# A feed-forward in two passes, its first product by seven block products, its middle layer in memory

## The chip, the cores and the metric

The kernel runs on one core of a Trainium2 chip. The metric is the device time of one execution in microseconds. The kernel before took 4279.12 us, the median of three runs (4273.91 to 4280.19).

## The reference, cut to what matters

The reference is a stack of two blocks of the first kind (layers 0 and 1) and one of a second kind with experts. 1024 tokens of width 1024 pass through all of them; 256 context tokens pass through layer 0. Everything is float32. A block of the first kind mixes the tokens (windowed attention, a gating unit, a Fourier mix, then the product with `w_out`), and ends in a feed-forward of width 4096. The scale, shift and gate vectors of each block come from a product of a condition vector with `w_ada`.

```
def squared_relu_mlp(h, w1, w2):
    return jnp.square(jax.nn.relu(h @ w1)) @ w2

for l in range(DEPTH):                      # DEPTH = 2
    mod_x = (silu(c) @ w_ada[l] + b_ada[l])
    sh1, sc1, g1, sh2, sc2, g2 = jnp.split(mod_x, 6, axis=-1)
    ...
    x = x + g1 * rmsnorm(y, g_post_mix[l])  # y: mixers, then @ w_out
    hx2 = rmsnorm(x, g_pre_ff[l]) * (1.0 + sc2) + sh2
    x = x + g2 * rmsnorm(squared_relu_mlp(hx2, w_ff1[l], w_ff2[l]), g_post_ff[l])
    # the same for the context h_ctx, in layer 0 alone
```

## The kernel before, in words

Every float32 matrix is split into a high part (`hi`, rounded to fp32r) and the rest (`lo`). A product is three matmuls: high by high, high by low, low by high (`mm3`). A split is a copy for `hi` (`copy` picks ScalarE or VectorE, `split` takes ScalarE) and a subtraction for `lo` (VectorE in `lo`; `lo_any` may pick GpSimd).

The order of all instructions on all engines is fixed at build time by a planner. Pieces of work are Python generators (`Sched.spawn`, with a priority; a lower number goes first); a `yield` of a condition holds a piece back until the planner's `Model` says that operands, buffers and banks are there. `Model` gives each instruction a time by a formula in `Engine.cost` (on VectorE 0.07 us and 0.00104 us per column, a DMA its bytes at 359 GB/s and 2 us). On the chip each engine then works through its list in that order and waits for semaphores; SP issues nearly all DMAs, also in order.

On-chip buffers: 46 blocks of 128x1024 float32 (`blk`), 7 half blocks (`hb`), 8 PSUM banks of 128x512. `room(n)`, `roomh(n)` and `banks(n)` ask whether n are free. `Weights` streams a list of weight tiles: load a block by SP, split it into two blocks, free the first.

`out_proj` multiplies each tile of 128 tokens by `w_out`, adds the residual, normalizes, transposes the result and stores the split transpose in `ffx`, the operand of the feed-forward: 4 row groups x 2 token halves x (hi, lo) = 16 blocks for the 1024 tokens, 4 for the context. When it is done, `ff` begins.

`ff` goes over groups of 128-column chunks of the middle layer (32 chunks; in layer 0 groups of two and a last one of four, in layer 1 groups of four). For each chunk and token half (512 tokens) it does 8 row blocks x 3 matmuls of 512 columns into one bank, and for the context 24 of 256 columns; `relu2` applies relu and square on ScalarE and splits the result into a block on the chip. Then, per token tile and 512 output columns, the group's chunks are multiplied by `w_ff2` into a bank, and VectorE adds the bank to an accumulator block. In the last group each finished tile goes to `finisher`: norm, residual, the next block's norm, transposes, split. The next block's input products follow at once.

`mod_dve` makes the modulation vectors that are needed later: a half of 512 columns is eight multiply-adds on VectorE for each of one or two vectors, with weights that SP loads into half blocks. It starts when layer 0's `out_proj` is over and runs beside the feed-forward.

Of the kernel before, what the change touches and what calls it, by code (L numbers as in the profile page):

```python
# [19 lines left out]
P = 128  # L20
# [12 lines left out]
FRES = 16  # L33
QLIM = 9
FLIM = 6
DEPTH = 3
# [10 lines left out]
GROUPS = [cuts(*[2]*14+[4]), cuts(*[4]*8)]  # L47
# [30 lines left out]
MG = 1  # L78
# [20 lines left out]
LB = 0.5  # L99
TP = 1  # L100
# [260 lines left out]
class Base:  # L361
    def __init__(self, ctx, tc, a):
        self.ctx, self.tc, self.a = ctx, tc, a
        self.m = Model()
        self.nc = NC(tc.nc, self.m)
        self.s = Sched(self.m)
        tp = lambda **k: ctx.enter_context(tc.tile_pool(**k))
        self.heap = tp(name="heap", bufs=1)
        self.small = tp(name="small", bufs=1)
        self.psum = tp(name="psum", bufs=NBANK, space=bass.MemoryType.PSUM)  # L370
        self.dram = tp(name="dram", bufs=1, space=bass.MemoryType.DRAM)
        self.rsv = 0
        self.bias = BIAS
        self.lbias = LB
        self.fstage = self.routing = 0
        self.slots = dict(blk=[0.0] * NBLK, hb=[0.0] * NHB, ps=[0.0] * NBANK)
# [226 lines left out]

class Seq:
# [11 lines left out]
class Block1(Base):  # L616
# [827 lines left out]
    def ff_dst(self, S, t):  # L1444
        X = S.ffx
        def dst(half):
            if S.ctx:
                return [(slice(0, 512), X[half][0][:, :, t * P:(t + 1) * P], X[half][1][:, :, t * P:(t + 1) * P])]
            out = []
            for i in range(2):  # L1450
                hi, lo = X[2 * half + i][t // 4]
                c = (t % 4) * P
                out.append((slice(i * 256, (i + 1) * 256), hi[:, :, c:c + P], lo[:, :, c:c + P]))
            return out
        return dst

    def out_proj(self, seqs, W, l, src, dst):
# [34 lines left out]
        def back(i, x, ys):  # L1492
            S, t = tiles[i]
            yield lambda: S.ctx in par
            G, A, B = par[S.ctx]
            yield from self.post(x, ys, G)
            self.unbank(*ys)
            nc.sync.dma_start(dst[S.ctx][t * P:(t + 1) * P, :], x)
            yield lambda: self.room(1)
            z = yield from self.prenorm(x, A, B)  # L1500
            self.free(x)
            S.odone += 1
            if S.odone == S.n:
                self.free(G, A, B)
            yield lambda: S.ctx or S.ffx[0][t // 4] is not None
            yield from self.transpose_split(z, self.ff_dst(S, t))
            self.free(z)
            S.ffdone.add(t)

        def halves():  # L1510
            for i in range(2):
                yield lambda: self.room(8 if dropped else 15) and (dropped if i else X.fourd)
                for kp in X.ffx:
                    kp[i] = tuple(self.blk((P, 2, 512), F32R) for _ in range(2))
# [4 lines left out]
        for i, (S, t) in enumerate(tiles):  # L1519
            if t == 0:  # L1520
# [3 lines left out]
                else:  # L1524
                    if len(seqs) == 2:
                        self.s.spawn(params(S), 1, "params")
                    S.ffx = [[None, None] for _ in range(4)]
# [16 lines left out]
        yield lambda: X.ffx[0][1] is not None  # L1544
# [3 lines left out]
    def ff_items(self, l, groups):  # L1548
        w1, w2 = self.a["w_ff1"][l], self.a["w_ff2"][l]
        it = []  # L1550
        for r in groups:
            it += [(("1", c), w1[:, c * P:(c + 1) * P].rearrange("(k p) f -> p k f", p=P), (P, KC, P)) for c in r]
            it += [(("2", c), w2[c * P:(c + 1) * P, :], (P, 1024)) for c in r]
        return it

    def relu2(self, ps, n, out, done, key):
        nc = self.nc
        yield lambda: self.roomh(1)
        r = self.hb()
        nc.scalar.activation(r[:, :n], ps[:, :n], AF.Relu)  # L1560
        self.unbank(ps)
        nc.scalar.activation(r[:, :n], r[:, :n], AF.Square)
        yield
        self.copy(out[:, 0, :n], r[:, :n])
        yield
        self.lo(out[:, 1, :n], r[:, :n], out[:, 0, :n])
        self.freeh(r)
        done.add(key)

    def ff(self, seqs, W, groups, fin, last_group):  # L1570
# [4 lines left out]
        need = lambda r: 2 * len(r) + (len(r) // 2 if C else 0)  # L1575
        yield lambda: self.room(10 if C else 8)
        acc = {(S.ctx, t): self.blk() for S in seqs for t in range(S.n)}
        done = set()
        self.ff_acc = 0
        hs = self.ff_h  # L1580
        for g, cs in enumerate(groups):
            last = g == len(groups) - 1
            parts = [(0, 0), (0, 1)] + ([(1, 0)] if C else [])
            order = [(c, p) for c in cs for p in parts] if g else [(c, p) for p in parts for c in cs]
            uses = {c: 0 for c in cs}
            for c, p in order:
                S, hb = seqs[0] if p[0] else X, p[1]
                nt = range(4 * hb, 4 * hb + 4) if not S.ctx else range(2)
                hk = (c - c % 2, "c") if S.ctx else (c, hb)
                yield lambda: W.has(("1", c)) and self.banks(2) and (hk in hs or self.room(1)) and all(t in S.ffdone for t in nt)  # L1590
                w1 = W.ready["1", c]
                ps = self.bank()
                if hk not in hs:
                    hs[hk] = self.blk((P, 2, 2, 256) if S.ctx else (P, 2, 512), F32R)
                h = hs[hk][:, c % 2] if S.ctx else hs[hk]
                n = 256 if S.ctx else 512
                for k in range(KC):
                    xh, xl = (x[:, k % 4, :] for x in S.ffx[k // 4]) if S.ctx else (x[:, k % 2, :] for x in S.ffx[k // 2][hb])
                    self.mm3(ps[:, :n], (w1[0][:, k, :], w1[1][:, k, :]), (xh, xl), k == 0, k == KC - 1)
                    if k % 4 == 3:  # L1600
                        yield 0
                self.s.spawn(self.relu2(ps, n, h, done, (c, p)), 0, "relu2")
                uses[c] += 1
                if uses[c] == len(parts):
                    W.drop(("1", c))
            if last:
                for S in seqs:
                    for kp in S.ffx:
                        for p_ in kp if not S.ctx else [kp]:
                            self.free(*p_)  # L1610
                last_group()
            else:
                self.ff_need = need(groups[g + 1])
            for S in reversed(seqs) if not last else seqs:
                if last:
                    yield from fin[S.ctx][0]()
                for t in range(S.n):
# [3 lines left out]
                    p = (1, 0) if S.ctx else (0, t // 4)  # L1621
                    av = acc[S.ctx, t]
                    for h in range(2):
                        yield lambda: W.has(*[("2", c) for c in cs]) and self.banks(2) and all((c, p) in done for c in cs)
                        ps = self.bank()
                        for i, c in enumerate(cs):
                            w2 = W.ready["2", c]
                            hb_ = hs[c - c % 2, "c"][:, c % 2] if S.ctx else hs[c, t // 4]
                            q = (t if S.ctx else t % 4) * P
                            self.mm3(ps, (hb_[:, 0, q:q + P], hb_[:, 1, q:q + P]), (w2[0][:, h * 512:(h + 1) * 512], w2[1][:, h * 512:(h + 1) * 512]),  # L1630
                                     i == 0, i == len(cs) - 1)
                        yield
# [8 lines left out]
                    if S.ctx and t == 1:  # L1641
                        self.free(*[hs.pop((c, "c")) for c in cs if c % 2 == 0])
                    elif t % 4 == 3:
                        self.free(*[hs.pop((c, t // 4)) for c in cs])
            W.drop(*[("2", c) for c in cs])

    def finisher(self, S, l, src, dst, nxt):
# [17 lines left out]
        def finish(t, ys, acc):  # L1665
# [7 lines left out]
            self.free(x)  # L1673
            yield lambda: self.room(2)
# [205 lines left out]
    def mods(self, X):  # L1880
# [4 lines left out]
        if MG & 1: yield lambda: self.fstage > 0  # L1885
# [12 lines left out]
    def block1(self, X, C):  # L1898
# [4 lines left out]
        for l in range(2):  # L1903
# [13 lines left out]
            self.ff_acc = 8 if last else 10  # L1917
            self.ff_h, self.ff_need = {}, 2 * len(groups[0]) + (0 if last else len(groups[0]) // 2)
            F = Weights(self, self.ff_items(l, groups), reserve=lambda: self.ff_need - len(self.ff_h) + self.ff_acc if X.outd else FRES)

# [7 lines left out]
            self.gmix = self.bc(a["g_mix"][l:l + 1, :])  # L1928
            s.spawn(F.task(), 2, "w")
# [19 lines left out]
            yield from self.ff(seqs, F, groups, fin, last_group)  # L1949
# [1426 lines left out]
```

## Time and profile before

| | |
|---|---|
| Runs | 4280.19, 4279.12, 4273.91 us, median 4279.12 |
| Profiled execution | 4273.9 us, span 4272.1 us, mean granted TensorE clock 0.973 |
| TensorE busy | 4026.4 us, 94% |
| VectorE, ScalarE, GpSimd busy | 2620.3 us (61%), 1776.9 us (42%), 552.9 us (13%) |
| HBM traffic | 488.42 MB read, 60.97 MB written, 129 GB/s over the span |

In the page PE is TensorE's matmuls, PEld its weight loads, DVE VectorE, ACT ScalarE, POOL GpSimd, SP the engine that issues DMAs. Nearly all instructions carry line L185, that of the helper that records them, so groups are told apart by operation, tiles and shape. The digits show 40 equal slices of the span, each 106.8 us; 9 is 90% or more busy. The feed-forward of layer 0 lies about from 640 to 1600 us, that of layer 1 from 2040 to 2770 us, and the block with the experts from there to the end.

### The profile page before, as it was taken

Reading aid. Unit: us, or ns where it says so; the run is one execution under the profiler, and the core shown is the slowest. Engines: PE = TensorE matmul, PEld = TensorE weight load, DVE = VectorE, ACT = ScalarE, POOL = GpSimd, SP = SyncE. Lnnn points to the kernel's source line nnn. Section 1 sums busy time; section 2 is a strip of 40 time slices with the busy share of each in tenths; the row PEclk is TensorE's granted clock in tenths of the full one; section 3 lists DMA queues with packets and bytes.
Section 4 is the critical chain, followed back from the end, with each engine's and each line's share of the span. In section 5 each row is a group of like instructions: output and inputs, shape, how many; then the busy total and the mean of one; then the engine's idle time right before and its main releaser. Section 6 shows DMA issues by size and latency. Waiting matters only on the chain. (4 is left out here: it accounts for less than half of the span.)

```text
span 4272.1 us, 54181 instructions
## 1 busy us (share of the span) xinstructions
PE 4026.4 (94%) x19792; PEld 3240.1 (76%) x19792; DVE 2620.3 (61%) x4945; ACT 1776.9 (42%) x3648; POOL 552.9 (13%) x723
## 2 busy tenths in 40 slices
PE   7998999999999989989999999799999999799997
PEld 3777777878888868878888888688666787587776
DVE  6447865666666486787333333733454677888998
ACT  3235644112222133474322112322454653677876
POOL 2112130000000052212000000401111124000001
PEclk8999999999999989999999999899999999899999
DMA  6212232233334141042211111421421356799998
GB/s 223 78 35 80 99 107 84 86 94 121 121 115 133 55 170 47 22 134 73 86 45 45 48 43 54 147 87 43 134 47 34 79 143 211 280 346 375 380 372 305
DMA packets 322917, 552.94 MB, mean 129 GB/s; under 512 B 101373, under 2 KB 181525, under 8 KB 322650
## 3 DMA queue, kind: packets, MB, share of 16 engines
q1 hardware_dynamic: 313290, 515.39, 35.5%
q0 software_dynamic: 9360, 34.08, 2.8%
q8 instruction: 156, 2.56, 0.2%
q14 instruction: 111, 0.91, 0.1%
HBM read 488.42 MB, written 60.97 MB: 129 GB/s over the span
## 5 line engine op out<-in xcount | busy, mean ns | idle before, releaser
L185 PE MATMUL ps<-blk 128*128 128x512 f32 (+3 forms) x16104 | 3569.8, 380 | 55.3 <-DVE blk L185 25.6
L185 PEld LDWEIGHTS ps<-blk 128*128 128x128 f32 (+1 forms) x16104 | 2825.5, 190 | 677.6 <-issue 95.4
L185 DVE TENSOR_TENSOR blk<-blk 128x1024 fp32r<-128x1024 f32 (+8 forms) x743 | 815.4, 1139 | 142.0 <-ACT blk L185 135.7
L185 ACT CAST blk<-blk 128x1024 fp32r<-128x1024 f32 (+2 forms) x625 | 608.1, 1025 | 658.6 <-DMA blk<-in_w_ff_dram 370.2
L185 DVE TENSOR_TENSOR blk<-blk,ps 128x512 f32<-128x512 f32 (+1 forms) x488 | 323.9, 676 | 325.2 <-PE ps L185 324.0
L185 ACT CAST blk<-ps 128x512 fp32r<-128x512 f32 (+4 forms) x610 | 276.8, 482 | 423.2 <-PE ps L185 404.7
L185 PE MATMUL ps<-ident,blk 128*128 128x128 f32 (+1 forms) x2024 | 321.6, 293 | 113.1 <-DVE blk L185 54.5
L185 DVE TENSOR_TENSOR blk<-ps,blk 128x512 fp32r<-128x512 f32 (+7 forms) x702 | 350.0, 533 | 114.6 <-ACT blk L185 88.5
L185 PEld LDWEIGHTS ps<-ident,blk 128*128 128x128 f32 x2024 | 257.4, 158 | 177.3 <-DVE blk L185 51.2
L185 POOL TENSOR_TENSOR blk<-blk 128x1024 f32<-128x1024 f32 (+3 forms) x113 | 240.1, 2129 | 1050.4 <-PE ps L185 664.6
L185 ACT ACTIVATE hb<-ps 128x512 f32<-128x512 f32 (+2 forms) x194 | 106.6, 549 | 521.0 <-PE ps L185 510.6
L185 DVE SCALAR_TENSOR_TENSOR hb<-hb,cT 128x512 f32<-128x512 f32 x224 | 164.3, 749 | 113.7 <-DMA hb<-in_w_ada_dram 112.2
L185 ACT ACTIVATE blk<-blk,z 128x256 f32<-128x256 f32 (+2 forms) x406 | 214.7, 533 | 44.0 <-DVE z L185 38.7
L185 DVE CAST blk<-hb 128x512 fp32r<-128x512 f32 (+3 forms) x130 | 49.8, 387 | 260.2 <-ACT hb L185 255.6
L185 ACT ACTIVATE hb<-hb 128x512 f32<-128x512 f32 (+5 forms) x386 | 176.1, 483 | 37.8 <-DVE hb L185 16.8
L185 ACT ACTIVATE blk<-ps 128x512 f32<-128x512 f32 (+1 forms) x198 | 116.6, 597 | 178.1 <-PE ps L185 173.2
L185 ACT ACTIVATE blk<-blk 128x1024 f32<-128x1024 f32 (+4 forms) x157 | 117.3, 750 | 170.1 <-DVE blk L185 142.6
L185 ACT COPY blk<-ps 128x512 f32<-128x512 f32 (+2 forms) x135 | 79.9, 598 | 242.1 <-PE ps L185 242.1
L185 DVE SCALAR_TENSOR_TENSOR blk<-blk,z 128x1024 f32<-128x1024 f32 (+2 forms) x146 | 157.1, 1110 | 21.9 <-POOL z L185 21.0
L185 DVE CAST blk<-ps 128x512 fp32r<-128x512 f32 (+3 forms) x176 | 91.5, 539 | 105.7 <-ACT blk L185 53.2
L185 DVE TENSOR_REDUCE mmx<-ps 128x1 f32<-128x512 f32 x128 | 81.6, 682 | 114.2 <-PE ps L185 114.0
L185 DVE TENSOR_TENSOR blk<-hb,blk 128x512 fp32r<-128x512 f32 (+5 forms) x224 | 122.1, 557 | 39.4 <-ACT blk L185 36.5
(146 smaller groups left out, 1701.3 us busy)
## 6 DMA issues: line engine op xcount, KB each, us to landing
blk<-in_w_ff_dram SPq DMA_DIRECT2D x128, 512.0 KB
blk<-in_w_gate_dram SPq DMA_DIRECT2D x128, 512.0 KB
blk<-in_w_up_dram SPq DMA_DIRECT2D x128, 512.0 KB
blk<-in_w_down_dram SPq DMA_DIRECT2D x128, 512.0 KB
hb<-in_w_ada_dram SPq DMA_DIRECT2D x208, 256.0 KB
blk<-in_w_ada_dram SPq DMA_DIRECT2D x40, 512.0 KB
blk<-in_w_in_dram SPq DMA_DIRECT2D x36, 512.0 KB
xd<-blk SPq DMA_DIRECT2D x32, 512.0 KB
```

Source lines behind the costliest of these rows:

```text
L185: return f(*a, **k)
```

## The change

The first product is done by seven block products in place of eight. The operand of 1024 tokens x 1024 rows is cut into four blocks (tokens 0 to 511 and 512 to 1023, rows 0 to 511 and 512 to 1023), `w_ff1` for a pair of chunks (p, p + 16) likewise. Sums of blocks are multiplied, and sums of the products give the four blocks of the result.

- `ff_combine` makes five further operand blocks for tokens 512 to 1023 in place of their plain transposes; `ffx` grows from 16 to 28 blocks (a, c, d, 1, 2, 3, 4).
- `Pairs` replaces `Weights` for `w_ff1`: it loads column p once for the first pass, then columns p and p + 16 for the second, makes four sums of 512 columns a pair (`two` picks VectorE or GpSimd) and splits them.
- The first pass (`ff_first`, priority 5) does two products a pair, and needs tokens 0 to 511 alone. One of them is kept in memory (`sd`).
- The second pass (`ff_second`) does the other five a pair, at most two pairs at a time in the half blocks, and adds the products on VectorE.
- `relu2` writes the split middle layer to memory (`hd`), and `ff_hidden` reads it back for the second product.
- The second product runs after that in groups of 1, then six of 2, then 3 pairs (2, 4 and 6 chunks), in both layers.
- `mod_dve` waits while the two passes run (`ffa`).
- `finisher` waits 4 us of the planner's time (`FS`) before the transposes.

```diff
-GROUPS = [cuts(*[2]*14+[4]), cuts(*[4]*8)]
+GROUPS = [cuts(1, *[2]*6, 3), cuts(1, *[2]*6, 3)]
+FS = 4.0
...
+    def two(self, out, x, y, op):
+        n, c = size(out), self.m.clk
+        if max(c["POOL"], self.m.now) + n * 0.0022 < max(c["DVE"], self.m.now) + n * 0.00104 + WB:
+            self.nc.gpsimd.tensor_tensor(out=out, in0=x, in1=y, op=op)
+        else:
+            self.nc.vector.tensor_tensor(out, x, y, op=op)
...
+class Pairs:
+    def load(self):
+        for p, j in self.order():
+            yield lambda: len(self.staged) < LEAD and self.room(1) and K.m.clk["DMA"] <= K.m.now + DQ
+            t = K.blk((P, KC, P))
+            c = p + 16 * (j == 2)
+            K.nc.sync.dma_start(t, self.w1[:, c * P:(c + 1) * P].rearrange("(k p) f -> p k f", p=P))
...
+    def rest(self, p):
+        yield lambda: self.arrived(p, 1) and self.arrived(p, 2) and self.room(1)
+        t, u = self.staged[p, 1][0], self.staged[p, 2][0]
+        lo, hi = slice(0, 4), slice(4, 8)
+        s = K.blk((P, KC, P))
+        K.two(s[:, hi], u[:, lo], u[:, hi], ad)
+        yield 0
+        K.two(s[:, lo], s[:, hi], t[:, lo], sb)
...
+        self.both((p, 1), s)
+        K.two(t[:, hi], t[:, hi], s[:, lo], sb)
...
+            self.half((p, 4), u[:, lo])
+        K.two(u[:, lo], t[:, lo], u[:, lo], sb)
...
+        self.both((p, 2), u)
...
+        self.half((p, 3), t[:, hi])
...
-                yield lambda: self.roomh(6)
+                yield lambda: self.roomh(6) and not self.ffa
...
+    def ff_combine(self, S, t, z):
...
+        for i in range(2):
+            hi, lo = (x[:, :, c].bitcast(F32) for x in S.ffx["a"][i])
+            tt(v(t1, i), v(pb, i), hi, op=OP.subtract)
+            tt(v(t1, i), v(t1, i), lo, op=OP.subtract)
...
+        tt(t2, pd, t1, op=OP.subtract)
...
+        self.copy(t3, pb)
+        for i in range(2):
+            hi, lo = (x[:, :, c].bitcast(F32) for x in S.ffx["c"][i])
+            tt(v(t4, i), hi, v(t2, i), op=OP.subtract)
+            tt(v(t4, i), v(t4, i), lo, op=OP.add)
...
+        tt(t3, pd, t3, op=OP.subtract)
...
+    def relu2(self, src, free, out, dst, n, p):
+        r = out[:, 1].bitcast(F32)
+        nc.scalar.activation(r, src, AF.Relu)
+        free(src)
+        nc.scalar.activation(r, r, AF.Square)
+        yield
+        self.copy(out[:, 0], r)
+        yield
+        self.lo(out[:, 1], r, out[:, 0])
+        yield
+        nc.sync.dma_start(dst, out.bitcast(F32))
...
+    def ff_pair(self, X, C, W, p, first, s1, v=None, w_=None):
...
+        def prod(j, o, b):
+            yield lambda: self.banks(2)
+            ps = got[0] = self.bank()
+            w = W.parts((p, j))
+            for k in range(4):
+                xh, xl = X.ffx[b][k // 2]
+                self.mm3(ps, (w[0][:, o + k], w[1][:, o + k]), (xh[:, k % 2], xl[:, k % 2]), k == 0, k == 3)
...
+        if first:
+            yield from prod(0, 0, "a")
+            go(snap(got[0]))
...
+            yield from prod(0, 4, "c")
+            go(final(s1, got[0], s1, 0))
+            return
+        nc.sync.dma_start(s1, self.sd[p])
+        yield from prod(1, 0, "2")
+        go(plus("u", s1, got[0], s1))
+        yield from prod(1, 4, "1")
+        m5 = got[0]
+        yield from prod(2, 0, "3")
+        go(plus("v", v, got[0], s1))
...
+        go(two())       # s1 + m5, then + v: one block of the result
+        yield from prod(2, 4, "4")
+        go(final(v, got[0], v, 2))
+        yield from prod(3, 0, "d")
+        go(final(s1, got[0], s1, 1))
...
+    def ff_second(self, seqs, W):
+        for p in range(16):
+            yield lambda: W.has((p, 1)) and self.banks(2) and self.roomh(3) and len(X.ffdone) == X.n and p in self.swhen and self.swhen[p] <= self.m.now
+            self.s.spawn(self.ff_pair(X, C, W, p, False, self.hb(), self.hb(), self.hb()), 5, f"pair{p}")
...
+    def ff_hidden(self, seqs, groups, W1, W2):
+        for g, r in enumerate(groups):
+            for part in self.ff_parts(seqs, g == len(groups) - 1):
+                for p in r:
...
+                    t = self.blk((P, 2, 2, 256), F32R)
+                    for i in range(2):
...
+                        self.nc.sync.dma_start(t[:, i].bitcast(F32), src)
...
             self.free(x)
+            yield FS
             yield lambda: self.room(2)
             yield from self.make_xT(S, t, z)
...
-        if MG & 1: yield lambda: self.fstage > 0
+        if MG & 1: yield lambda: self.fstage > 0 and not self.ffa
...
+            F = Pairs(self, a["w_ff1"][l], not last, reserve=lambda: ARES if X.outd else FRES if "a" in X.ffx else 16)
+            E = Weights(self, self.ff_items(l, groups), reserve=lambda: 4 if F.ns == 16 else ER, gate={"2": lambda: F.nl == 48})
...
+            self.ffa = True
+            s.spawn(self.ff_first(seqs, F), 5, "ff1")
             yield from self.out_proj(seqs, O, l, (self.xd[1] if last else a["x"][0], a["ctx"][0]), (self.xd[2 * l], self.cd))
...
+            s.spawn(E.task(), 2, "w")
```

## Rows read from the trace of the kernel before

**Rows 1.** The page: busy time by engine, and slices of the span.
```profile
PE 4026.4 (94%) x19792; PEld 3240.1 (76%) x19792; DVE 2620.3 (61%) x4945; ACT 1776.9 (42%) x3648; POOL 552.9 (13%) x723
...
PE   7998999999999989989999999799999999799997
...
GB/s 223 78 35 80 99 107 84 86 94 121 121 115 133 55 170 47 22 134 73 86 45 45 48 43 54 147 87 43 134 47 34 79 143 211 280 346 375 380 372 305
```

**Rows 2.** Busy time by window: us, each engine's busy (instructions), clock, DMA share, GB/s.
```profile
2100.00:2600.00 500.00, 500.00 (x2208) 414.01 (x2207) 156.95 (x213) 112.84 (x156) 0.00 (x0) 1.00 0.16 50
1550.00:1600.00 50.00, 35.93 (x162) 29.08 (x160) 49.19 (x55) 17.99 (x42) 38.94 (x40) 0.87 0.39 135
2700.00:2750.00 50.00, 44.29 (x204) 35.77 (x202) 45.21 (x51) 18.63 (x44) 34.18 (x39) 0.97 0.40 128
2750.00:2800.00 50.00, 30.55 (x127) 25.26 (x128) 40.02 (x69) 22.51 (x31) 14.96 (x11) 0.73 0.36 120
2030.00:2050.00 20.00, 17.06 (x74) 13.67 (x74) 15.02 (x24) 9.40 (x19) 4.88 (x6) 0.83 0.55 159
640.00:660.00 20.00, 13.62 (x54) 10.01 (x53) 16.33 (x30) 8.81 (x20) 3.27 (x3) 0.74 0.32 104
```

**Rows 3.** Groups by shape, 2100 to 2600 us: count, busy us, mean ns, idle before.
```profile
L185 PE MATMUL ps<-blk 128*128 128x512 f32 x2208 | 500.6, 389 | 0.0
...
L185 DVE TENSOR_TENSOR blk<-blk 128x1024 fp32r<-128x1024 f32 x47 | 56.5, 1223 | 54.4 <-ACT blk L185 54.4
L185 DVE TENSOR_TENSOR blk<-blk,ps 128x512 f32<-128x512 f32 x80 | 55.0, 687 | 146.2 <-PE ps L185 146.2
L185 ACT CAST blk<-blk 128x1024 fp32r<-128x1024 f32 x47 | 48.9, 1045 | 185.8 <-PE ps L185 185.8
L185 DVE TENSOR_TENSOR blk<-hb,blk 128x512 fp32r<-128x512 f32 x46 | 31.7, 688 | 19.4 <-ACT blk L185 18.8
...
L185 DVE CAST blk<-hb 128x512 fp32r<-128x512 f32 x40 | 17.1, 427 | 133.9 <-ACT hb L185 133.9
```

**Rows 4.** Groups by shape, 700 to 1400 us.
```profile
L185 PE MATMUL ps<-blk 128*128 128x256 f32 x576 | 73.3, 284 | 0.0
...
L185 ACT CAST blk<-blk 128x1024 fp32r<-128x1024 f32 x48 | 50.5, 1051 | 360.8 <-DMA blk<-in_w_ff_dram 335.8 <-DVE blk L185 24.5 <-PE ps L185 0.5
```

**Rows 5.** TensorE's waits (us, times, longest): 1500 to 1650 us first, then 2700 to 2800.
```profile
PE ps L185 <- DVE blk L185: 18.4, 5, 14.7
...
PE ps L185 <- POOL blk L185: 13.5, 1, 13.5
PE ps L185 <- DVE blk L185: 10.4, 3, 7.4
```

**Rows 6.** Groups by shape over the whole span, GpSimd and VectorE.
```profile
L185 POOL TENSOR_TENSOR blk<-blk 128x512 f32<-128x512 f32 x19 | 25.4, 1336 | 140.6 <-DVE blk L185 82.7 <-DVE hb L185 37.6 <-PE ps L185 9.4
...
L185 DVE SCALAR_TENSOR_TENSOR hb<-hb,cT 128x512 f32<-128x512 f32 x224 | 164.3, 749 | 113.7 <-DMA hb<-in_w_ada_dram 112.2
...
L185 DVE TENSOR_TENSOR blk<-ps,blk 128x256 f32<-128x256 f32 x32 | 11.9, 415 | 0.0
```

**Rows 7.** Groups by shape, 1540 to 1620 us, VectorE.
```profile
L185 DVE TENSOR_TENSOR blk<-blk 128x1024 fp32r<-128x1024 f32 x5 | 9.7, 1949 | 0.0
L185 DVE TENSOR_TENSOR blk<-blk,ps 128x512 f32<-128x512 f32 x14 | 9.5, 675 | 0.0
```

**Rows 8.** DMA issues: count, KB each, median us from issue to landing.
```profile
blk<-in_dftx_hi_dram POOLq DMA_DIRECT2D x16, 512.0 KB, 4.5
```

**Rows 9.** The DMA queue's timeline at four modulation halves: start, us, operation.
```profile
788.31 4.12 SPq L185 DMA_DIRECT2D mod<-hb  x2
...
834.36 4.11 SPq L185 DMA_DIRECT2D mod<-hb  x2
...
1025.63 0.24 SPq L185 DMA_DIRECT2D mod<-hb  x1
...
1050.08 0.24 SPq L185 DMA_DIRECT2D mod<-hb  x1
```

More of the change, by code (lines that the diff above doesn't have):

```diff
@@ L99 @@
 LB = 0.5
+WB = 0.3
+FS = 4.0
+ER = 9
 TP = 1
@@ L1448, in dst @@
                 return [(slice(0, 512), X[half][0][:, :, t * P:(t + 1) * P], X[half][1][:, :, t * P:(t + 1) * P])]
[L1449 to L1454, printed above, removed]
-        return dst
+            return [(slice(i * 256, (i + 1) * 256), hi[:, :, t * P:(t + 1) * P], lo[:, :, t * P:(t + 1) * P])
+                    for i, (hi, lo) in enumerate(X["c" if half else "a"])]
@@ L1504, in back @@
                 self.free(G, A, B)
[L1505 to L1507 removed]
+            if S.ctx or t < 4:
+                yield lambda: S.ctx or "a" in S.ffx
+                yield from self.transpose_split(z, self.ff_dst(S, t))
+                self.free(z)
+            else:
+                yield lambda: "d" in S.ffx and t - 4 in S.ffdone
+                yield from self.ff_combine(S, t, z)
             S.ffdone.add(t)
         def halves():
[L1511 to L1514, printed above, removed]
+            for i, nms in enumerate(("ac", "d1234")):
+                yield lambda: self.room(4 * len(nms) if dropped else 15) and (dropped if i else X.fourd)
+                for nm in nms:
+                    X.ffx[nm] = [tuple(self.blk((P, 2, 512), F32R) for _ in range(2)) for _ in range(2)]
         self.s.spawn(params(seqs[0]), 1, "params")
@@ L1543, in out_proj @@
         dropped.append(1)
-        yield lambda: X.ffx[0][1] is not None
+        yield lambda: "d" in X.ffx
         X.outd = True
     def ff_items(self, l, groups):
[L1549 to L1556, printed above, removed]
-        nc = self.nc
[L1558 to L1562, printed above, removed]
+        w2 = self.a["w_ff2"][l]
@@ new lines, in ff_first @@
+    def ff_first(self, seqs, W):
+        X = seqs[-1]
+        C = seqs[0] if len(seqs) == 2 else None
+        for p in range(16):
+            yield lambda: W.has((p, 0)) and self.banks(PBANK) and self.roomh(1) and all(t in X.ffdone for t in range(4))
+            yield from self.ff_pair(X, C, W, p, True, self.hb())
+    def ff_second(self, seqs, W):
+        X = seqs[-1]
+        C = seqs[0] if len(seqs) == 2 else None
+        self.ffp = 0
+        for p in range(16):
+            yield lambda: W.has((p, 1)) and self.banks(2) and self.roomh(3) and len(X.ffdone) == X.n and p in self.swhen and self.swhen[p] <= self.m.now
+            self.s.spawn(self.ff_pair(X, C, W, p, False, self.hb(), self.hb(), self.hb()), 5, f"pair{p}")
+            yield 0.3
+        yield lambda: self.ffp == 16
+        for nm in X.ffx:
+            for x in X.ffx[nm]:
+                self.free(*x)
+        if C:
+            for x in C.ffx:
+                self.free(*x)
+        self.ffa = False
@@ L1574, in ff @@
         C = seqs[0] if len(seqs) == 2 else None
[L1575 to L1581, printed above, removed]
-            last = g == len(groups) - 1
[L1583 to L1605, printed above, removed]
@@ L1606, in ff @@
+        self.hl = {}
+        self.s.spawn(self.ff_hidden(seqs, groups, W1, W), 2, "hidden")
+        yield from self.ff_second(seqs, W1)
+        acc = {}
+        for g, r in enumerate(groups):
+            last = g == len(groups) - 1
+            cs = [c for p in r for c in (p, p + 16)]
             if last:
[L1607 to L1610, printed above, removed]
                 last_group()
-            else:
-                self.ff_need = need(groups[g + 1])
@@ L1614, in ff @@
-            for S in reversed(seqs) if not last else seqs:
-                if last:
+            for part in self.ff_parts(seqs, last):
+                S = C if part == 4 else X
+                if last and part in (0, 4):
                     yield from fin[S.ctx][0]()
-                for t in range(S.n):
+                keys = [(p, part) for p in r]
+                here = lambda: all(k in self.hl and self.hl[k][1] <= self.m.now + SLACK for k in keys)
+                for t in range(2) if S.ctx else range(2 * part, 2 * part + 2):
@@ L1620, in ff @@
                         fin[S.ctx][1](t)
-                    p = (1, 0) if S.ctx else (0, t // 4)
+                    if g == 0:
+                        yield lambda: self.room(1)
+                        acc[S.ctx, t] = self.blk()
                     av = acc[S.ctx, t]
+                    q = t % 2 * P
                     for h in range(2):
-                        yield lambda: W.has(*[("2", c) for c in cs]) and self.banks(2) and all((c, p) in done for c in cs)
+                        yield lambda: W.has(*[("2", c) for c in cs]) and self.banks(2) and here()
                         ps = self.bank()
@@ L1640, in ff @@
                         self.s.spawn(fin[S.ctx][2](t, [av[:, 0:512], av[:, 512:1024]], av), 0, f"fin{t}")
[L1641 to L1644, printed above, removed]
+                self.free(*[self.hl.pop(k)[0] for k in keys])
             W.drop(*[("2", c) for c in cs])
```

209 lines of the change are left out of this document (195 added, 14 removed).

## The prediction

> **What bounds the kernel now.** I read the page first, for the engine that is busy most and for where its slices fall. TensorE is busy 94% of the span; its digits are 9 through two long plateaus, the feed-forwards, with dips around them [rows 1]. Then the table of windows, to see who is full in each stage. Inside a feed-forward TensorE has no idle time at the full clock while VectorE is 31% busy (156.95 of 500 us). At the end of both feed-forwards it turns round: VectorE 49.19 of 50 us and TensorE 35.93 at the first, VectorE 45.21 then 40.02 and TensorE 44.29 then 30.55 at the second, with granted clocks down to 0.87 and 0.73. Two smaller dips stand where the feed-forwards begin, at 640 and 2030 us [rows 2]. Third, groups of instructions by shape in the second plateau: 2208 matmuls in 500.6 us with 0.0 idle, so 226.7 ns each [rows 3]. So TensorE bounds both feed-forwards, VectorE the two ends. A removed matmul is worth its full 226.7 ns as long as VectorE, which gets the block sums, stays under TensorE's pace.
>
> **Removed matmuls.** The first product of the 1024 tokens is 32 column chunks x 2 token halves x 8 row blocks x 3 (high-high, high-low, low-high) = 1536 matmuls a layer. Seven block products of eight leave 16 pairs x 7 x 4 x 3 = 1344. 192 fewer in each of two layers, 384 x 226.7 ns = **87.1 us**, with nothing beside them that would stay. The context's matmuls and the second product keep their number.
>
> **First pass** (two products a pair, and the combining of tokens 512 to 1023 in out_proj). TensorE per pair: 24 x 226.7 ns = 5.4 us, in layer 0 plus 24 matmuls of 256 columns at 73.3/576 = 0.127 us [rows 4] = 8.5 us; 16 pairs are 87 us in layer 1 and 136 in layer 0. VectorE per pair: a split's difference 1.22, one sum from PSUM 0.69, one difference of the hidden tile 0.69, half of the casts 0.2 [rows 3]: 2.8 us, with the context's 256 columns 3.3; 16 pairs 45 and 53 us. Combining a tile costs VectorE four 256-column differences from PSUM and from SBUF each (8 x 0.42 = 3.3), two of 512 (1.4), ten low halves of 256 (4.2) and about half of eleven casts (1.5), at 415 ns for 256 columns [rows 6]: 10.4 us, four tiles 42 us. So VectorE has 87 us of work in layer 1's first pass of 87 us, and 95 in layer 0's 136. Against that, the pass needs only tokens 0 to 511: it fills the dips at 640 and 2030 us, where 20-us windows hold 54 and 74 matmuls of 88 possible (20/0.2267), or (34 + 14) x 0.2267 = 11 us together. That is partly transposes. I take -3 for both layers: 8 gained in layer 0, 5 lost in layer 1. Ends: -11 (both filled) and +20 (the 42 us of combining half exposed in layer 1).
>
> **Second pass** (five products a pair). TensorE per pair 60 x 0.2267 = 13.6 us, in layer 0 16.7 with the context. VectorE per pair, at the durations of [rows 3]: six sums from PSUM 4.1, two splits 2.4, one half split 0.7, three hidden differences 2.1, three casts 1.3 = 10.6 us; layer 0 adds a half split and the context, 1.4 = 12.0. Then four weight combinations of 512 columns, 0.69 us each on VectorE, or 1.34 on POOL [rows 6]. If VectorE takes all it has 13.4 of 13.6 us in layer 1 and 14.8 of 16.7 in layer 0; if POOL takes all, 78% and 72%. The cover is thin. The order is also written by a model that holds 512 columns on VectorE at 0.07 + 512 x 0.00104 = 0.60 us where the trace has 0.69, so on the chip VectorE runs late against the plan. Eight banks let it lag by several products (2.7 us each) before TensorE waits. POOL's work isn't free: beside it a 1024-column difference takes 1.95 us, not 1.22, while the same engine's sums from PSUM stay at 0.675 [rows 7]; each overlap adds 0.73. With all combinations on VectorE and two 1024- and four 512-column differences overlapped, VectorE would have 13.4 + 2 x 0.73 + 4 x 0.37 = 16.3 us in layer 1 (2.7 over) and 17.7 in layer 0 (1.0 over): +60 us. Below, nothing. I take 0.5 us a pair, +16, nearer the free end, because VectorE's plain sum is under TensorE's in both layers.
> The Trainium skill ("SBUF — State Buffer", section "Who interferes with whom") goes further than the row: a VectorE instruction with two SBUF inputs and a GpSimd instruction that reads SBUF exclude each other for the whole instruction. By that rule four combinations on POOL would shut VectorE's differences out for 4 x 1.34 = 5.4 us of a pair, 16.0 us against 13.6 in layer 1: +38 us there, inside the ends above.
>
> **Memory traffic.** Added per layer: the hidden layer written and read back, 16 x 2 MB each way plus 16 x 0.5 MB each way for the context in layer 0; the first sums, 16 x 0.25 MB each way; 16 column loads of 0.5 MB repeated. Densest is layer 1's second pass: 2 loads, 3 hidden tiles and a sum per pair, 2.9 MB in 13.6 us = 212 GB/s, under the 380 that the page's slices reach [rows 1]. I cost it at nothing, with these 43% as room; what it could do is delay, which is a rival below.
>
> **Handover to the second product.** The first group now has one pair, whose hidden tiles come from memory. A 512 KB load took 4.5 us from issue to landing [rows 8]. One load not hidden per layer: 4 us each, **+8**. Ends 0 and 20 (two loads in a row).
>
> **The modulation vectors.** They were made by VectorE beside all of layer 0's feed-forward; now they wait until its second pass is over. Halves with two vectors stand 46 us apart, with one 25 us [rows 9]. The last group of layer 0 needs six two-vector halves, 276 us, and the seven groups before it last 13/16 x 1920 x 0.2267 = 354 us, so it isn't late. The rest (20 halves, 500 us) goes on into layer 1's mixers and second product. The work is 224 x 0.75 = 164 us [rows 6] moved from under a full TensorE to stages where it is partly seen. I take **+8**; ends 0 and 25.
>
> **Ends of the feed-forwards.** The last group goes from four chunks to six: 36 matmuls a tile, 8.2 us, in place of 24, 5.4. VectorE's work on a finished tile is the same, so 8 x 2.72 = 21.8 us of matmuls move under VectorE's full stretch, in each layer. TensorE waits there 18.4 us for VectorE in the first, 10.4 for VectorE and 13.5 for POOL in the second [rows 5]; the lower clock comes on top (0.73 over 50 us is up to 13 us of full-speed time, partly within the waits). The 4-us pause ahead of the transposes keeps them from standing in TensorE's queue before their input. I take 13 each, **-26**, as some modulation work falls here and the last tile's chain stays. Ends 0 and -44.
>
> **Sum.** -87 - 3 + 16 + 8 + 8 - 26 = -84. The profiled execution took 4273.9 us (its span 4272.1), so 4190. The median of the three runs is 4279.1, 5 us above it.
>
> **The rivals.**
> 1. VectorE sets the second pass's pace: +60 in place of +16, 4234. For it: 98% without POOL, and 1.95 us in place of 1.22 with it. Against: eight banks of slack, and an idle time of 0.0 in both plateaus [rows 3, 4].
> 2. More is gained: both ends close (-44), no stall in the second pass: 4190 - 18 - 16 = 4156. For it: at the ends VectorE is the full engine [rows 2]. Against: the last tile's chain remains in any order.
> 3. Slower: the weights of the second pass arrive too late. 28 buffers hold the token blocks (4 more the context), so 14 to 18 of 46 are left, and a pair's two loads wait for buffers of the pair before. Load 4.5, two combinations 1.4, cast 1.05, difference 1.2: 8.2 us from issue to the first matmul, which nothing covers if the buffers come free only at the pair's end. The model takes 3.5 us for the load; ScalarE already waited 335.8 us at 48 splits, 7.0 each, for such loads [rows 4]. Half exposed, 32 x 4.1 = 131 us: 4190 - 16 + 131 = 4305. It decides from 3.1 us a pair ((84 + 16)/32) on. Against: four loads may be under way, and the buffers of a pair come free product by product.
> 4. Nothing: the saved matmuls turn into stalls elsewhere (first pass +20, second +60, handover +20, modulation +25, ends -26): +12, 4286.
>
> **Chances.** Forecast 0.50, rival 1 0.20, rival 2 0.15, rival 3 0.13, rival 4 0.02. A measurement of this kernel tells about 0.2%, 8.5 us, from nothing. Faster: 0.50 + 0.15 + 0.17 of rival 1, 0.82. Same: 0.02 of rival 1's upper tail and rival 4, 0.04. Slower: rival 3 and 0.01 of rival 1's tail, 0.14. The range 4130 to 4265 holds all but rival 3 and the tails: its low end is -87 - 11 - 44, its high end rival 1 with the handover and the modulation at their ends.
>
> **What the changed profile would show.** 384 fewer matmuls of 128x512; the spacing inside the second pass still 227 ns with VectorE under 95%; no TensorE waits over 3 us in it; the two end windows with fewer than 25 us of waits. TensorE waiting once a pair on ScalarE's or VectorE's split would be rival 3, short waits on PSUM banks rival 1. The prediction is wrong if TensorE has idle time spread through the second pass.

## The result, and the profile after

The changed kernel took 4209.16 us, the median of four runs (4206.42 to 4219.34), against 4276.51 for the kernel before beside it: ratio 0.9849, interval 0.9827 to 0.9871. Its profiled execution has a span of 4205.0 us, 67.1 less than before. The forecast was 4190: the sign is right, and 67 of the 84 us forecast came. The time is 19 us above the forecast and inside its range.

The page after, the line that answers to [rows 1]:

```profile
PE 3952.7 (94%) x19408; PEld 3173.7 (75%) x19408; DVE 2777.8 (66%) x5162; ACT 1905.1 (45%) x3884; POOL 704.5 (17%) x841
```

TensorE has 384 instructions fewer and is 73.7 us less busy; VectorE is 157.5 us busier. The windows that answer to [rows 2], in order of time but for the last: the first passes (650, 2000), the handover in layer 0, where the second pass ends and the second product begins (1050), the ends of layer 0 (1450, 1500) and of layer 1 (2650), and layer 1's second pass (2100 to 2250):

```profile
650.00:700.00 50.00, 44.20 (x243) 37.73 (x242) 47.62 (x96) 33.51 (x75) 5.59 (x4) 0.90 0.45 143
...
1050.00:1100.00 50.00, 46.22 (x206) 37.94 (x205) 27.48 (x35) 28.86 (x43) 0.00 (x0) 0.97 0.95 324
...
1450.00:1500.00 50.00, 39.59 (x170) 32.05 (x170) 33.28 (x35) 10.31 (x26) 24.71 (x26) 0.86 0.57 205
1500.00:1550.00 50.00, 39.54 (x189) 31.28 (x187) 46.70 (x59) 15.10 (x37) 22.07 (x31) 0.98 0.46 155
...
2000.00:2050.00 50.00, 42.42 (x174) 34.41 (x174) 48.05 (x96) 33.74 (x71) 5.64 (x4) 0.92 0.43 138
...
2650.00:2700.00 50.00, 37.25 (x167) 28.25 (x166) 41.87 (x61) 17.13 (x39) 17.64 (x27) 0.88 0.50 166
...
2100.00:2250.00 150.00, 150.00 (x664) 124.20 (x663) 123.44 (x138) 87.68 (x136) 69.80 (x46) 1.00 0.71 223
```

The second pass is as full as the old plateau: 664 matmuls in 150 us, 226 ns each, VectorE 82% busy. What is lost lies at the starts and the ends. TensorE's waits that answer to [rows 5], 1440 to 1600 us first, then 2600 to 2750:

```profile
PE ps L194 <- POOL blk L194: 20.5, 4, 9.9
PE ps L194 <- DVE hb L194: 3.8, 2, 3.1
PE ps L194 <- DVE blk L194: 2.1, 2, 1.3
...
PE ps L194 <- POOL blk L194: 8.5, 1, 8.5
PE ps L194 <- DVE blk L194: 6.8, 4, 3.1
```

In the kernel before, the stretch at the end of layer 0 (1500 to 1650 us) had, beside the 18.4 us for VectorE of [rows 5]:

```profile
PE ps L185 <- POOL blk L185: 5.2, 2, 4.0
```

So at the end of layer 0 the waits are as long as before, and GpSimd has taken VectorE's place in them; at the end of layer 1 they are shorter.

To compare stages that differ in length I summed, over the matmuls of each trace, how much later the next one starts than is usual behind a matmul of the same shape and tiles (the 20th percentile of these in that trace). That is matmul time lost to idle and to the lower clock, in us:

| kernel | start of layer 0 | end of layer 0 | mixers of layer 1 | start of layer 1 | end of layer 1 | whole span |
|---|---|---|---|---|---|---|
| before | 12.1 | 37.8 | 38.4 | 7.3 | 32.5 | 431.0 |
| after | 13.7 | 38.2 | 43.6 | 17.4 | 24.0 | 447.6 |
| e2_short | 13.6 | 18.1 | 39.0 | 17.0 | 17.9 | 421.2 |
| e6_pool_lo | 12.0 | 38.1 | 45.2 | 14.1 | 24.3 | 448.4 |
| e8_early | 13.7 | 21.3 | 44.2 | 17.5 | 23.1 | 434.4 |
| e9_dve_add | 13.7 | 24.3 | 45.2 | 17.1 | 22.5 | 432.7 |
| e13_best | 12.5 | 18.0 | 40.1 | 11.4 | 16.8 | 414.2 |
| e14_dve_before | 12.3 | 24.0 | 35.9 | 5.9 | 19.8 | 413.6 |

The stages are, in the kernel after, 625 to 700, 1425 to 1600, 1600 to 1900, 1900 to 2050 and 2600 to 2750 us, and the same in its variants; in the kernel before and its variant 625 to 700, 1500 to 1650, 1650 to 1950, 1950 to 2050 and 2650 to 2800.

### The profile page after: what moved, and what is told of

Read it like the earlier page. It is cut to its first block, busy times and chain, and to the rows that moved or that the text cites. A ratio compares the mean times of both kernels' runs of the same rounds, so it can differ in the third digit from the quotient of the medians.

```text
span 4205.0 us, 55307 instructions
## 1 busy us (share of the span) xinstructions
PE 3952.7 (94%) x19408; PEld 3173.7 (75%) x19408; DVE 2777.8 (66%) x5162; ACT 1905.1 (45%) x3884; POOL 704.5 (17%) x841
## 3 DMA queue, kind: packets, MB, share of 16 engines
q14 instruction: 126, 1.03, 0.1%
## 5 line engine op out<-in xcount | busy, mean ns | idle before, releaser
L194 PE MATMUL ps<-blk 128*128 128x512 f32 (+6 forms) x15720 | 3488.4, 380 | 58.8 <-DVE blk L194 25.7
L194 PEld LDWEIGHTS ps<-blk 128*128 128x128 f32 (+3 forms) x15720 | 2758.1, 191 | 664.4 <-issue 91.1
L194 DVE TENSOR_TENSOR blk<-blk 128x1024 fp32r<-128x1024 f32 (+6 forms) x993 | 1007.9, 1055 | 175.2 <-ACT blk L194 159.5
L194 ACT CAST blk<-blk 128x1024 fp32r<-128x1024 f32 (+3 forms) x831 | 731.8, 933 | 505.9 <-PE ps L194 230.0
L194 POOL TENSOR_TENSOR blk<-blk 128x512 f32<-128x512 f32 (+3 forms) x231 | 400.5, 1741 | 1220.4 <-DVE blk L194 357.5
L194 ACT CAST blk<-ps 128x512 fp32r<-128x512 f32 (+5 forms) x598 | 274.0, 485 | 430.6 <-PE ps L194 404.3
L194 DVE TENSOR_TENSOR blk<-blk,ps 128x512 f32<-128x512 f32 (+1 forms) x348 | 230.2, 671 | 241.1 <-PE ps L194 240.5
L194 ACT ACTIVATE blk<-blk 128x512 f32<-128x512 f32 (+4 forms) x317 | 211.6, 669 | 362.0 <-DVE blk L194 301.9
L194 DVE TENSOR_TENSOR hb<-ps,hb 128x512 f32<-128x512 f32 (+4 forms) x281 | 186.7, 674 | 133.3 <-PE ps L194 106.7
L194 ACT ACTIVATE blk<-ps 128x512 f32<-128x512 f32 (+2 forms) x230 | 128.8, 567 | 278.8 <-PE ps L194 271.9
```

What stands on the lines that cost most here:

```text
L194: return f(*a, **k)
```

## The experiments

Medians stand beside 4209.16 of the changed kernel and 4276 to 4279 of the one before; ratios are to the kernel before. The four runs of the changed kernel alone lie within 13 us, so two medians of its family within 10 us are not told apart.

**What a product is worth, and whether the second pass has slack.** e1_eight:

```diff
         yield from prod(3, 0, "d")
+        m7 = got[0]
+        yield from prod(3, 0, "d")
+        self.unbank(got[0])
+        got[0] = m7
```

> The changed kernel with an eighth product in each pair of the second pass: product d is done a second time into a bank that nobody reads (12 matmuls a pair, 384 in all, as many as the change removed). Theory: TensorE is full through the second pass and VectorE is not, so all of it shows: 384 x 0.2267 = +87 us, about 4296, above the kernel before. Rival: VectorE or the weights set the pace of the pass and TensorE has hidden slack; then much of the 87 us fits into it, +20 to +60.

4288.05 us, ratio 1.002 (1.001 to 1.0029): 79 us more than the changed kernel, of 87. The pass has no slack for a product; with its matmuls put back the change is worth nothing, so the matmuls removed are its gain. Of the 8 us that are missing some 6 are the handover of layer 0. With the longer pass it comes some 40 us later, and nothing is lost in it (windows 1050 to 1150 us):

```profile
1050.00:1100.00 50.00, 50.00 (x245) 42.34 (x244) 25.37 (x38) 25.19 (x42) 1.68 (x1) 1.00 0.56 200
1100.00:1150.00 50.00, 50.00 (x219) 40.48 (x218) 31.11 (x38) 22.20 (x30) 0.00 (x0) 1.00 0.81 280
```

In the kernel after, the handover's window (1050 to 1100 us) has TensorE 46.22 us busy, at 324 GB/s.

**Whether VectorE is at the edge there.** e11_nopool sets `WB = -9.0`.

> The changed kernel with all weight combinations on VectorE (WB -9, so two never takes GpSimd). In layer 1's second pass VectorE is 41.5 of 50 us busy and GpSimd 23 to 26. Theory (VectorE has slack in the second pass, as the forecast had it): VectorE goes to about 95% and TensorE stays full: within 8 us of 4209. Rival 1 of the prediction (VectorE is at the edge): it passes 100%, TensorE waits on banks, +15 to +45 us, nearly all in layer 1's second pass.

4218.32 us, ratio 0.9865 (0.985 to 0.988): 9 us more, which is not told apart from the changed kernel (and 1 us over what the theory allowed). TensorE has no wait between 2050 and 2320 us. The window of 150 us in its second pass, and behind it the handover of layer 1:

```profile
2100.00:2250.00 150.00, 150.00 (x663) 124.20 (x662) 127.79 (x192) 76.40 (x116) 0.00 (x0) 1.00 0.67 214
...
2300.00:2350.00 50.00, 45.50 (x194) 37.17 (x193) 27.10 (x39) 25.54 (x39) 0.00 (x0) 0.95 1.00 348
```

VectorE does 54 instructions more than in the kernel after (45 combinations and 14 casts more, 5 others fewer) and is busy 4.4 us more. So rival 1 falls, and GpSimd was hardly a help. Most of what this trace loses beyond the kernel after lies at the handover of layer 1; in the kernel after TensorE is full in that window. The groups of the kernel after in the same 150 us say why GpSimd helped so little:

```profile
L194 POOL TENSOR_TENSOR blk<-blk 128x512 f32<-128x512 f32 x46 | 70.1, 1535 | 80.3 <-DMA hd<-blk 40.5 <-DMA blk<-in_w_ff_dram 23.1 <-PE ps L194 15.1
L194 DVE TENSOR_TENSOR blk<-blk 128x512 fp32r<-128x512 f32 x45 | 46.0, 1032 | 4.3 <-ACT blk L194 4.0
L194 DVE TENSOR_TENSOR hb<-ps,hb 128x512 f32<-128x512 f32 x68 | 45.7, 684 | 17.0 <-PE ps L194 11.8 <-DMA sd<-hb 4.1
L194 DVE TENSOR_TENSOR blk<-blk 128x1024 fp32r<-128x1024 f32 x24 | 38.8, 1618 | 5.3 <-ACT blk L194 5.3
```

And those of e11_nopool:

```profile
L194 DVE TENSOR_TENSOR blk<-blk 128x512 fp32r<-128x512 f32 x44 | 28.1, 687 | 0.0
L194 DVE TENSOR_TENSOR blk<-blk 128x1024 fp32r<-128x1024 f32 x22 | 26.9, 1221 | 7.8 <-ACT blk L194 7.8
...
L194 DVE CAST blk<-blk 128x512 fp32r<-128x512 f32 x14 | 5.8, 421 | 0.0
```

46 combinations at 0.69 us would be 32 us of VectorE; but beside them its own differences take 1.03 us in place of 0.69 and 1.62 in place of 1.22, 45 x 0.34 + 24 x 0.40 = 25 us. Its sums from PSUM kept 0.684. Taken one by one, only the differences that overlap a GpSimd instruction are longer: 21 of 512 columns take 1.39 us on average and the other 23 take 0.68, 13 of 1024 columns take 1.96 and the other 11 take 1.21.

**What the modulation vectors cost in their new place.** e2_short, and e3_short_before as its control, leave out seven eighths of this work, its multiply-adds and its loads:

```diff
-                for k in range(n):
+                for k in range(1):
                     load(k)
                 yield
-                for k in range(KC):
+                for k in range(1):
...
-                    if k + n < KC:
+                    if k + n < 1:
```

> The changed kernel with modulation vectors that take one row block of eight (mod_dve's loop runs once; seven eighths of its multiply-adds and loads are left out). Theory: moved behind the passes they cost something at the end of layer 0 (23 multiply-adds, some 18 us of VectorE, lie in that full stretch) and in layer 1's mixers, where matmul time lost rose by 7 us: -12 to -20 us against the changed kernel, about 4192. Rival: they are hidden where they are, and the end of layer 0 is late for another reason (parameter loads, GpSimd's additions): within 5 us of 4209.

> The same cut of the modulation loop in the kernel before, as the control for e2_short. Both theories: there the work lies under a full TensorE, whose own matmuls are the bound, so nothing beyond -3 us against 4276.

e2_short 4182.19 us, ratio 0.9772 (0.9759 to 0.9785), 27 us less; e3_short_before 4278.85, ratio 1.0 (0.9991 to 1.0009). The work was free where it lay before and costs 27 us now: of the lost matmul time 20 us are gone at the end of layer 0 (38.2 to 18.1), 5 in layer 1's mixers and 6 at the end of layer 1. Not all of the 20 need be VectorE's time. The loads are left out too, and a parameter that holds up the end of layer 0 in the changed kernel (below) comes earlier: GpSimd is idle 0.3 us for it in the trace of e2_short, 15.2 in the kernel after.

**A faster pace for it.** e12_deep:

```diff
-                ws = [self.hb() for _ in range(3 - len(vs))]
+                ws = [self.hb() for _ in range(6 - len(vs))]
```

> The changed kernel with the modulation weights loaded deeper ahead: five or four half blocks for weights in place of two or one (ws has 6 - len(vs)), in the half blocks that the second product leaves free. All arithmetic stays. Theory: e2_short's 26 us are the halves' slow pace (46 and 25 us a half, waiting for one load after the other), which drags them into the end of layer 0 and into layer 1's mixers; with loads in flight all 26 halves fit under layer 0's second product, and most of the 26 us comes back: -15 to -25 us, about 4189. Rival: the work itself costs it, wherever it lies, or its loads crowd out the hidden tiles' loads: within 5 us of 4209.

4239.4 us, ratio 0.9909 (0.9895 to 0.9923): 30 us more, against the theory. A two-vector half took 30 us in place of 51 to 57, but 27 of the instructions still fell between 1460 and 1600 us, where the changed kernel has 24. The end of layer 0 lost 39.9 us, and the mixers of layer 1, which last until about 1950 us in this trace, lost some 84 where the changed kernel lost 43.6. Each half now holds six of the seven half blocks, which the mixers need too; that this is the cause was not tried by itself.

**Whether the larger last group helps.** e4_last4:

```diff
-GROUPS = [cuts(1, *[2]*6, 3), cuts(1, *[2]*6, 3)]
+GROUPS = [cuts(1, 1, *[2]*7), cuts(1, 1, *[2]*7)]
```

> The changed kernel with the last group of the second product at 2 pairs (4 chunks, as before the change) in place of 3 (groups 1, 1, then seven of 2). Theory: the larger last group put 8 x 2.72 = 22 us of matmuls a layer under VectorE's full stretch, of which the prediction booked 13 a layer: +26 us, 4235. Rival: the ends wait for things that a larger group doesn't help (GpSimd's additions, parameters that land late, as the trace after shows 20.5 us of TensorE waiting for GpSimd): within 8 us of 4209.

4231.1 us, ratio 0.9886 (0.9869 to 0.9903): 22 us more. TensorE's waits for GpSimd at the two ends are 24.2 and 21.6 us, where the kernel after has 20.5 and 8.5, and one for VectorE of 13.9 comes on top:

```profile
PE ps L194 <- POOL blk L194: 24.2, 4, 9.3
PE ps L194 <- DVE blk L194: 15.1, 3, 13.9
...
PE ps L194 <- POOL blk L194: 21.6, 4, 7.9
```

So the larger group is worth 22 us, near the 26 that the prediction booked for it.

**What took that gain back.** In the trace after, the finisher's parameters are loaded at the start of the last group, while the queues are at 386 GB/s (window 1460 to 1470). The timeline of SP and of GpSimd:

```profile
1458.02 0.42 SPq L194 DMA_DIRECT2D blk<-in_g_post_ff_dram  x1
...
1465.48 2.39 POOL L194 TENSOR_TENSOR blk<-blk 128x1024 f32<-128x1024 f32 x1 [15.22 <-DMA blk<-in_g_post_ff_dram]
```

From the load's issue to GpSimd's start 7.5 us pass, and what GpSimd has to do for the finisher stands behind it in its list. e8_early makes the parameters one group earlier:

```diff
+        begun = []
+        def begin(S):
+            yield from fin[S.ctx][0]()
+            begun.append(S.ctx)
         for g, r in enumerate(groups):
+            if g == len(groups) - 2:
+                for S in seqs:
+                    self.s.spawn(begin(S), 1, "begin")
...
-                    yield from fin[S.ctx][0]()
+                    yield lambda: S.ctx in begun
```

> The changed kernel with the finisher's gate, scale and shift loaded and made one group earlier (the same instructions, begun at the start of the last group but one). In the trace after GpSimd waits 15.2 us for g_post_ff at the end of layer 0 while the queue moves 386 GB/s. Theory A (the end of layer 0 gains nothing because the finisher starts late on its parameters): -5 to -10 us, 4201. Theory B (modulation work in that stretch, shown by e2_short, is what takes the gain): within 4 us of 4209.

4184.29 us, ratio 0.9778 (0.9762 to 0.9794): 25 us less, more than expected. The profiled execution is the slowest of the five, 17 us under that of the changed kernel, and the end of layer 0 loses 17 us less. TensorE no longer waits for GpSimd at the end of layer 0; its waits there sum to 12.2 us, where the kernel after has 26.4. The longest:

```profile
PE ps L194 <- DVE blk L194: 7.2, 3, 6.6
PE ps L194 <- ACT blk L194: 3.1, 1, 3.1
```

**GpSimd's additions in the finisher.** e9_dve_add, and e14_dve_before as its control:

```diff
-        self.add(z, z, B)
+        self.add(z, z, B, bias)
...
-            z = yield from self.prenorm(x, st["A"], st["B"])
+            z = yield from self.prenorm(x, st["A"], st["B"], -9.0)
```

`post` is changed in the same way. With -9.0 `add` never takes GpSimd.

> The changed kernel with all of the finisher's additions on VectorE and none on GpSimd. TensorE waits 20.5 us for GpSimd at the end of layer 0 and 8.5 at the end of layer 1. Theory: GpSimd is only the last link, VectorE has no room for the additions (1.2 us each, two a tile): slower by 5 to 15 us, 4219. Rival: GpSimd's 2.6 us and the stretched VectorE instructions beside it cost more than the additions: faster by 5 to 15 us, 4199.

> The finisher's additions all on VectorE in the kernel before, the control for e9_dve_add. Theory: there VectorE itself is full at the ends (TensorE waits 18.4 us for VectorE and 5.2 for GpSimd at layer 0's) with less matmul work to cover it, so its extra additions cost as much as they free: within 6 us of 4277. Rival: GpSimd's share in those ends is dear in either kernel, and the change's 15 us appear here too: 4262.

e9_dve_add 4193.79 us, ratio 0.9801 (0.9786 to 0.9817), 15 us less: its rival was right. e14_dve_before 4255.77, ratio 0.995 (0.9937 to 0.9964), 21 us less, against its theory: both ends of the kernel before lose 13 us less, though at the end of layer 0 VectorE was the engine most waited for. The additions of 128x1024 between 1460 and 1600 us, in the kernel after (one of GpSimd's eleven makes a parameter) and then in e9_dve_add:

```profile
L194 POOL TENSOR_TENSOR blk<-blk 128x1024 f32<-128x1024 f32 x11 | 28.5, 2594 | 28.8 <-DMA blk<-in_g_post_ff_dram 15.2 <-DVE blk L194 11.3 <-issue 2.3
...
L194 DVE TENSOR_TENSOR blk<-blk 128x1024 f32<-128x1024 f32 x9 | 13.0, 1442 | 0.1
...
L194 DVE TENSOR_TENSOR blk<-blk 128x1024 f32<-128x1024 f32 x19 | 22.9, 1217 | 0.0
```

An addition takes GpSimd twice as long as VectorE, and VectorE's own get shorter without GpSimd beside them. In the kernel before it is the same between 1500 and 1650 us: 13 additions at 2.5 us on GpSimd and 7 at 1.86 on VectorE; in e14_dve_before all 20 are on VectorE, at 1.22.

**The combining.** e6_pool_lo sets `CA = True`.

> The changed kernel with the low halves of the combined operand blocks free to go to GpSimd (CA true: ff_combine's splits use lo_any). Theory: the first passes lose 10 us more than the starts of the feed-forwards lost before because the combining fills VectorE there (47.6 and 48.1 of 50 us); with up to 13 us of differences off VectorE per layer the loss falls by 4 to 8 us, about 4203. Rival: GpSimd shares operand access with VectorE, so its differences slow VectorE's by as much as they take over: within 4 us of 4209, or a little above.

4206.23 us, ratio 0.9829 (0.9813 to 0.9846): not told apart. In the trace the starts lose 1.7 and 3.3 us less, as if the combining were part of the loss there; that is too little to settle it.

**The memory traffic.** e7_double issues each read of `hd` twice.

> The changed kernel with every read of the hidden layer done twice (75 MB more, in the two second products, where the queues now move 150 to 270 GB/s). Theory: the second product hides the traffic, but at its end, where 386 GB/s were reached, parameters and next weights land later still: +3 to +12 us, all of it at the two ends. Rival: traffic costs nothing that shows (the prediction's nothing): within 3 us of 4209. Second rival: the second product itself starves on hidden tiles: +20 us or more, spread over it.

4889.38 us, ratio 1.1436 (1.1418 to 1.1453): none of the theories (the second rival's size, but not for its reason), because the edit added a wait and not only bytes. The second read writes the same tile, so SP holds it until the first has landed. SP's waits:

```profile
SPq L194 <- DMA blk<-hd: 861.7, 288, 7.2
```

288 waits of 3.0 us on SP, 862 us in all, with all other loads behind them, became 680 us of time; part of it is the clock, granted at 0.911 in the mean where the kernel after has 0.971. What the added bytes alone cost stays open.

**Together.** e13_best is e8_early, e9_dve_add and e6_pool_lo in one.

> The changed kernel with e8_early, e9_dve_add and e6_pool_lo together. Theory: e8 and e9 cured the same loss at the end of layer 0 (38 us of lost matmul time there, 21 and 24 with either), by two links of one chain (GpSimd's queue stands behind a late parameter), so the gains don't add: 4175 to 4184. Rival: two separate losses, gains add: 4209 - 25 - 15 - 3 = 4166.

4170.89 us, ratio 0.9755 (0.9742 to 0.9768): 38 us under the changed kernel, of 43 if all gains added, so between the theory and its rival. At the end of layer 0 they don't add (18.0 lost; 21.3 and 24.3 with one each), at the end of layer 1 they do more than that (16.8; 23.1 and 22.5). It beats both kernels.

## Why the prediction was right, step by step

The sign, the gain's source and the full second pass are as worked out. Three terms of the sum are off by 15 us or more: the first pass and the modulation cost more, the second pass less. The errors go in both directions, so that the sum came within 17 us is in part luck.

- **Removed matmuls, -87.1.** Held: 384 fewer of 128x512, at 227 ns, and 79 us back when as many are put in again.
- **First pass, -3 (ends -11 and +20).** Wrong in sign: the two starts lose 31.1 us where they lost 19.4, +12. VectorE is at 47.6 and 48.1 of 50 us there, as the working had it for layer 1; the loss came in that layer, 10 of the 12. But TensorE's waits there (1960 to 2060 us) are 5.0 us for an addition on GpSimd, 2.5 for VectorE and 2.1 for ScalarE, so a full VectorE is not all of it, and how much is the combining was not shown.
- **Second pass, +16.** Too much: no wait at all in either layer. The working gave VectorE 13.4 of 13.6 us a pair without GpSimd; e11_nopool shows 127.8 of 150 us, 11.6 a pair. Some 0.7 of the 1.8 us are casts: the working put three a pair on VectorE, and the trace has 14 there in 11 pairs. The rest is that the working added up durations, and successive VectorE instructions overlap in the trace (140 us of durations in 128 of busy time). Its upper end, +60, could not come: it put all combinations on VectorE and yet had GpSimd stretch the differences, and GpSimd does nothing in that stretch of e11_nopool. The Trainium skill's rule ("SBUF — State Buffer", section "Who interferes with whom") agrees with the trace in direction: beside GpSimd's 70 us VectorE's differences took 25 us longer, and the 68 sums from PSUM no longer at all; the 5.4 us a pair worked out by it were not reached, the trace has 25 us in 11 pairs, 2.3 a pair.
- **Handover, +8.** 6.0 us lost at 1050 us in layer 0; layer 1 has no such loss. The size is near, the cause another: TensorE waited there not for a hidden tile from memory but for a split of 1024 columns, as the weights of the second product need it (3.0 us for ScalarE's cast, 0.8 for VectorE's difference).
- **Modulation, +8 (ends 0 and +25).** Undersized, and above its upper end: 27 us by e2_short against its control of 0. Nothing had to wait for it, as worked out (the six halves were done at 1388 us, at 51 to 57 us each in place of 46; the last group began near 1437); but it ran on into the finishing of layer 0, 24 of its instructions on VectorE in 1460 to 1600 us, 19 us. The step that was off is the price of work moved beside a full VectorE.
- **Ends, -26.** The group's size is worth 22 us, as e4_last4 shows. But the ends lose only 8 us less than before, because at the end of layer 0 the finisher starts late, and TensorE's waits there, 26.4 us, miss the sign of fewer than 25. e2_short, e8_early and e9_dve_add each take 14 to 20 of the 38 us away, and the last two together (in e13_best) 20: one loss with several links, a parameter that lands late, GpSimd's list behind it, and VectorE's modulation work between. The late parameter is not needed for all of it: in e9_dve_add GpSimd is idle 15.4 us for it, as in the kernel after, and 14 us are gained all the same. Which link counts most is not settled, and what the pause `FS` is worth no run shows.
- **Memory traffic at nothing.** Right for the second pass and the second product, which are full; not for the handover (324 GB/s) and probably not for the late parameters, though e8_early moves them in time and does not take traffic away.

By stage the errors are +15 in the first pass, -16 in the second, -2 at the handover, +18 at the ends (most of the modulation's 27 lies there) and -3 in layer 1's mixers (5 lost, 8 booked): +12 of the 17 us by which the profiled executions fell short of 84. Some 4 more were lost before 625 us (104.7 and 108.8 by the same sum), ahead of all that the change adds; variants of either kernel, the same up to there, lose 104 to 111, so executions differ by that much. Added up from experiments where there are any, the account is the same: -87 for the matmuls, -22 for the larger group (e4_last4), +27 for the modulation (e2_short), +12 and +6 at the starts and the handover (the traces) make -64, and -67 was measured. None of the rivals happened: the second pass has no wait for VectorE or for weights (1 and 3), the ends did not close (2), and the gain did not turn into stalls (4).

## What to carry to other kernels

Where an engine is full and has no slack, as e1_eight showed here, a cut of its work is worth nearly its time; what moves out from under it has a price of its own. Price each moved piece where it lands, above all beside another stage's full stretch. At the end of a stage look for the first instruction of the helper engine's list: a parameter loaded there holds up all that stands behind it, and here it could be made a group earlier at no cost that shows. Before work is given to GpSimd, count how much longer it makes VectorE's instructions on two SBUF operands beside it: here 25 of the 32 us moved.

## What the runs showed of the hardware that was not expected

GpSimd was hardly a relief for VectorE: with 46 combinations on it (32 us of VectorE's time) VectorE was busy only 4.4 us less in 150, because its differences beside them took 25 us longer. Keeping the finisher's additions off GpSimd made the kernel before 21 us faster too. And short waits in SP's list are dear: 288 of 3.0 us made the kernel 680 us longer.
